# Splitting the first load of x and of the weights in two, moving the load of the mix, and moving the retrieval's weight splits behind the last norm

## The chip, the cores and the metric

The kernel runs on one core of a Trainium2 chip. The metric is the device time in microseconds (us) of one execution; three timed runs of the kernel before the change are given below, with one profiled execution. Engines are named as in the profile: PE (TensorE), ACT (ScalarE), DVE (VectorE), POOL (GpSimd) and SP (SyncE, which here issues DMAs). PEld is the weight load of PE.

## What is computed

One decoder block for 512 tokens of width 1024, all in float32:

```
u = rms_norm(x, norm_mix_g)
z = u @ w_in                                   # 1024 x 3328
o = concat(diff_attention(z[:, :1536]), rwkv7_mix(z[:, 1536:]))
h = x + o @ w_out
q = rms_norm(h, norm_ffn_g) @ peer_w_q         # retrieval: 8 heads, 16 of 128 x 128 keys
h = h + sum over the 16 best experts of gate * gelu(u . exp_u) * exp_v
h = h + sigmoid(rms_norm(h, norm_ple_g) @ ple_gate_w) * (p @ ple_proj_w)
out = rms_norm(h, norm_final_g)
```

In `rwkv7_mix` the projected columns are first blended with those of the token before, `zs = z + (prev - z) * mu`; `mu` (rw_mu) is "the mix" of the change. `diff_attention` needs sine and cosine tables of the positions (the rotary tables).

## The kernel before

Matmuls work on pairs of fp32r tiles: every operand is split into `hi` (a rounded copy, made by ACT, line 133) and `lo` (the rest, made by DVE or POOL, line 143, or line 145 where a gain is multiplied in). A product is three matmuls: hi by hi, hi by lo, lo by hi (lines 217 to 219).

**The first projection.** `mixers` computes columns of z in groups of four token blocks at a time, contracting over eight blocks k of 128 rows. The groups come in the order k (512 columns), l (256 columns, the low-rank inputs), r, v, then the attention's columns. `proj_steps` takes weights from `stream`, which fetches two blocks k in one DMA of 512 KB into a raw tile (`wraw`, three buffers), splits them block by block into `whi` and `wlo` (two buffers of each, two blocks to a buffer) and yields them one after the other. In the first group x itself is still to be loaded: `columns(k)` loads two blocks of the transposed x (`xt`, 512 KB) and splits them into `uhi` and `ulo`; the list `begin` says after which block k the next such load, the squares of x and the row scales are written.

**The shift.** `shift_group` gets the results of a group: ACT copies each block out of PSUM with its row scale into `zz` (line 446), then SP issues two or three DMAs for each block (lines 455 to 460, 11 for a group) that shift it by one token, and POOL computes the blend in three instructions for each block (lines 461 to 464). `mu` is loaded when the group is set up (line 438), as one row that is written to all 128 partitions, 256 KB.

**The rotary tables.** `rope_tables` (lines 349 to 424) works on tiles of 128 x 32 with a long chain of small DVE instructions. `lambdas` (lines 330 to 346) makes two small DVE sums of four short loads (`lam`). Both are written after the groups k, l, r and v and have no order of their own.

**What sets the order.** The program is written in one order and a scheduler then gives every engine its own fixed list, by its own estimate of when inputs are ready. `behind(i, first)` holds instruction i after `first` on the same engine's list without a wait on the chip. An edit in one place can thus move instructions elsewhere. The queue of SP is one list too: a DMA whose buffer is not yet free holds up all behind it.

**The output projection and the norm.** `out_proj` multiplies by `w_out` (lines 253 to 255); after the last block's two halves `norm(b)` is called for the blocks: ACT squares (line 1061), DVE adds the two sums (1649), ACT takes the root (123), DVE the reciprocal (124) and the two halves of the normed rows `xn` (1653), PE transposes them (159), ACT and DVE split them into `u2hi` and `u2lo`. Then `retrieve` multiplies the weights `peer_w_q`, streamed in the same way, by them (lines 1113 to 1115). The first four pairs of its blocks are split by ACT and DVE, later ones by ACT and POOL.

## Time and profile before

| | us |
|---|---|
| median of 3 runs | 1800.03 |
| lowest and highest | 1797.09, 1800.13 |
| the profiled execution, its own time | 1795.69 |
| its span, first to last instruction | 1794.0 |
| PE busy in the span | 1691.8 (94%) |
| DVE busy | 1397.3 (78%) |
| ACT, POOL busy | 751.5, 647.3 |

The profiled execution lies 4.34 us under the median and 1.7 us over its own span. Times in rows are from the start of the span. The stretch from 0 to about 111 us is the projection of the groups k, l, r, v and the first attention columns, 400 to 455 us the output projection and the norm, 455 to 600 us the retrieval, and the rest the experts.

### The profile page before, as it was taken

To read this page: it belongs to the slowest core of one execution; us is meant where nothing else is said; L and a number is where in the kernel's file an instruction comes from. 1 tells how busy PE (TensorE), PEld (TensorE's weight loads), DVE (VectorE), ACT (ScalarE), POOL (GpSimd) and SP (SyncE) were. 2 spreads that over 40 slices of the span, in tenths; PEclk is the share of its full clock that TensorE was granted. 3 is DMA by queue.
4 is the path that set the end of the run, shared out by engine and by line. 5 is a ranking of instruction groups with operands and counts; after the bars stand their busy time and mean duration, and the time that the engine had idled before them with its cause. 6 is when DMAs were issued, how large, how long until landed. Compare 5 with 4: busy or idle time off the path is not lost.

```text
span 1794.0 us, 30877 instructions
## 1 busy us (share of the span) xinstructions
PE 1691.8 (94%) x11642; PEld 1447.2 (81%) x11642; DVE 1397.3 (78%) x3004; ACT 751.5 (42%) x1358; POOL 647.3 (36%) x574
## 2 busy tenths in 40 slices
PE   7899978989889879999999999999999999999998
PEld 5767667667677879997777888888999989989986
DVE  5486858774499979878888888888888888888785
ACT  5345523343456654444444333333333333333363
POOL 3460120212278840001111233335545455555520
PEclk9899966899999989999999999999999999999999
DMA  7444353414522434455665677778989898989881
GB/s 230 147 128 118 106 130 87 111 27 165 188 82 81 139 102 132 137 188 198 210 208 190 221 267 235 262 266 299 315 301 316 301 319 301 313 308 315 304 321 47
DMA packets 150426, 363.86 MB, mean 203 GB/s; under 512 B 43922, under 2 KB 58510, under 8 KB 150148
## 3 DMA queue, kind: packets, MB, share of 16 engines
q1 hardware_dynamic: 113412, 227.65, 38.9%
q0 software_dynamic: 36864, 134.23, 22.1%
q8 instruction: 91, 1.49, 0.3%
q14 instruction: 59, 0.48, 0.1%
HBM read 332.61 MB, written 21.36 MB: 197 GB/s over the span
## 4 chain that ended last, share of the span: by engine, by line
PE 67%; DVE 24%; ACT 4%; issue 2%; DMA 2%; POOL 1%; SPq 0%; DVEq 0%; ACTq 0%; POOLq 0%
PE po L1395 22%; PE phid L1253 9%; PE phid L1255 9%; PE phid L1254 8%; PE pg L1364 3%; ACT whi L133 2%; DVE wlo L143 2%; PE acc L217 2%; PE acc L218 2%; PE acc L219 2%; DVE ids L1202 1%; DVE rest L1079 1%; DVE sol_p L630 1%; DVE wlo L145 1%; DVE jj L1352 1%
## 5 line engine op out<-in xcount | busy, mean ns | idle before, releaser
L143 DVE TENSOR_TENSOR wlo<-wraw,whi 128x1024 fp32r<-128x1024 f32 x245 | 299.6, 1223 | 144.7 <-ACT whi L133 144.6
L133 ACT ACTIVATE whi<-wraw 128x1024 fp32r<-128x1024 f32 x276 | 291.4, 1056 | 166.6 <-PE phid L1254 68.5
L1253 PE MATMUL phid<-u2dhi,whi 128*128 128x384 f32 x1024 | 349.1, 341 | 5.7 <-ACT row L1262 5.7
L1255 PE MATMUL phid<-u2dhi,wlo 128*128 128x384 f32 x1024 | 346.1, 338 | 5.5 <-POOL wlo L143 5.5
L1254 PE MATMUL phid<-u2dlo,whi 128*128 128x384 f32 x1024 | 345.6, 338 | 0.0
L1418 POOL DMA_INDIRECT row<-in_peer_u_dram,idx x128 | 190.0, 1485 | 408.0 <-DVE row L1430 219.4
L1418 POOL DMA_INDIRECT row<-in_peer_v_dram,idx x128 | 186.0, 1453 | 276.3 <-DVE h L1434 194.4
L1395 PE MATMUL po<-whi,clo 128*128 128x512 f32 x768 | 243.1, 398 | 1.4
L1395 PE MATMUL po<-whi,chi 128*128 128x512 f32 x768 | 243.3, 398 | 1.2 <-ACT row L1262 1.2
L1395 PE MATMUL po<-wlo,chi 128*128 128x512 f32 x768 | 241.4, 395 | 0.0
L1253 PEld LDWEIGHTS phid<-u2dhi,whi 128*128 128x128 f32 x1024 | 193.5, 189 | 10.8 <-ACT row L1262 6.6
L1255 PEld LDWEIGHTS phid<-u2dhi,wlo 128*128 128x128 f32 x1024 | 193.4, 189 | 6.1 <-POOL wlo L143 6.1
L1254 PEld LDWEIGHTS phid<-u2dlo,whi 128*128 128x128 f32 x1024 | 193.7, 189 | 3.7
L1395 PEld LDWEIGHTS po<-whi,clo 128*128 128x128 f32 x768 | 143.0, 188 | 41.9 <-DVE clo L145 8.7
L1395 PEld LDWEIGHTS po<-wlo,chi 128*128 128x128 f32 x768 | 144.4, 188 | 33.6
L133 ACT ACTIVATE chi<-gelu 128x384 fp32r<-128x384 f32 x128 | 67.3, 526 | 240.6 <-DVE gelu L1372 121.4
L1434 DVE SCALAR_TENSOR_TENSOR h<-row,ids,h 128x1024 f32<-128x1024 f32 x128 | 163.9, 1280 | 1.5
L1395 PEld LDWEIGHTS po<-whi,chi 128*128 128x128 f32 x768 | 140.9, 188 | 25.6 <-ACT row L1262 1.5
L1262 ACT ACTIVATE gelu<-phid 128x384 f32<-128x384 f32 x86 | 42.4, 493 | 266.4 <-PE phid L1255 244.8
L1430 DVE SCALAR_TENSOR_TENSOR row<-row,xn 128x1024 f32<-128x1024 f32 x128 | 153.6, 1219 | 0.0
L143 POOL TENSOR_TENSOR wlo<-wraw,whi 128x1024 fp32r<-128x1024 f32 (+1 forms) x46 | 80.0, 1752 | 111.3 <-ACT whi L133 111.3
L218 PE MATMUL acc<-wlo,uhi 128*128 128x512 f32 (+1 forms) x224 | 89.7, 401 | 10.7 <-DVE wlo L145 10.7
(452 smaller groups left out, 2866.1 us busy)
## 6 DMA issues: line engine op xcount, KB each, us to landing
wraw<-in_peer_uT_dram SPq DMA_DIRECT2D x128, 512.0 KB
wraw<-in_peer_v_dram SPq DMA_DIRECT2D x128, 512.0 KB
wraw<-in_w_in_dram SPq DMA_DIRECT2D x24, 512.0 KB
wraw<-in_peer_w_q_dram SPq DMA_DIRECT2D x16, 512.0 KB
ahead<-row SPq DMA_DIRECT2D x42, 192.0 KB
gelu<-ahead SPq DMA_DIRECT2D x42, 192.0 KB
wraw<-in_w_out_dram SPq DMA_DIRECT2D x8, 512.0 KB
zz<-zz SPq DMA_DIRECT2D x12, 224.0 KB
```

The costliest lines, as they stand in the source:

```text
L133: self.last_hi = nc.scalar.activation(hi, src, AF.Copy, **({} if g is None else {"scale": g}))
L143: self.last_lo = eng.tensor_tensor(lo[s], src[s], hi[s].bitcast(F32), op=OP.subtract)
L218: nc.tensor.matmul(o, hi[:, k, s], wlo, start=False, stop=False)
L1253: nc.tensor.matmul(ps, whi[:, s], hi[:, k, :], start=(k == 0), stop=False)
L1254: nc.tensor.matmul(ps, whi[:, s], lo[:, k, :], start=False, stop=False)
L1255: nc.tensor.matmul(ps, wlo[:, s], hi[:, k, :], start=False, stop=(k == KC - 1))
L1262: nc.scalar.activation(g, ps, AF.Gelu)
L1364: nc.tensor.matmul(ps[:, t], jj[:, t], gi[:, i, t], start=i == 0, stop=i == 1)
L1395: nc.tensor.matmul(outs[b, e], lhs[:, s], rhs[:, 512 * e:512 * e + 512], start=(c == 0 and rhs is vhi and lhs is chi), stop=(c == NKEY - 1 ...
L1418: nc.gpsimd.indirect_dma_start(out=row, out_offset=None, in_=a["peer_u" if kind == "U" else "peer_v"], in_offset=bass.IndirectOffsetOnAxis ...
L1430: nc.vector.scalar_tensor_tensor(row, row, 1.0, xn0, op0=OP.mult, op1=OP.mult, accum_out=hid0[:, k:k + 1])
L1434: nc.vector.scalar_tensor_tensor(acc0, row, hid0[:, k:k + 1], acc0, op0=OP.mult, op1=OP.add)
```

## The change

Three edits. (1) For the first pair of blocks alone, x and the weights are loaded as two DMAs of 256 KB each instead of one of 512 KB, and x is split block by block: the first half of x before the product of block 0, the second after it. (2) The load of `mu` for the first group is written later, after the row scales; for the other groups it stays where it was. (3) In `out_proj` the norm of block 2 is written behind the last half product instead of ahead of it, and in `retrieve` the splits of the first three pairs of weight blocks are held behind the last block's norm: ACT's part behind its square root, DVE's part behind the last half of `xn`.

```diff
@@ rms
-        nc.scalar.activation(r, ss, AF.Sqrt, bias=self.eps, scale=1.0 / D)
+        self.rooted = nc.scalar.activation(r, ss, AF.Sqrt, bias=self.eps, scale=1.0 / D)
@@ fetch
-        i = self.nc.sync.dma_start(raw[:, :n] if len(src.shape) == 2 else
-                                   raw[:, :n].rearrange("p (k n) -> p k n", k=src.shape[1]), src)
+        if not self.fetches:
+
+            for k in range(2):
+                m = n // 2
+                i = self.nc.sync.dma_start(raw[:, k * m:k * m + m], src[:, k])
+        else:
+            i = self.nc.sync.dma_start(raw[:, :n] if len(src.shape) == 2 else
+                                       raw[:, :n].rearrange("p (k n) -> p k n", k=src.shape[1]), src)
@@ shift_group
-        nc.sync.dma_start(mu[:, :n], bcast_row(self.a["rw_mu"][:, g0:g0 + n], n))
+
+        def load_mu():
+            nc.sync.dma_start(mu[:, :n], bcast_row(self.a["rw_mu"][:, g0:g0 + n], n))
...
-        return zs, consume
+        return zs, consume, load_mu
@@ mixers
-            columns(0)
-            begin = {0: [lambda: columns(2)], 2: [lambda: columns(4)], 4: [lambda: columns(6)],
+
+            xt0 = self.p4("xt", [128, 2, T])
+
+            def column(k):
+                nc.sync.dma_start(xt0[:, k], a["xT"][k * 128:k * 128 + 128, :])
+                self.split(hi[:, k], lo[:, k], xt0[:, k])
+            column(0)
+            begin = {0: [lambda: column(1), lambda: columns(2)], 2: [lambda: columns(4)], 4: [lambda: columns(6)],
...
+                if zs:
+                    load_mu()
+                else:
+                    begin[7].append(load_mu)
@@ out_proj
-                            for x in ((0, 1, 2), (3,))[i]:
+                            for x in ((0, 1), (2, 3))[i]:
@@ retrieve
+                        if cg == 0 and k in (2, 4):
+
+                            self.behind(self.last_hi, self.rooted)
+                            self.behind(self.last_lo, self.normed)
@@ norm
-                    nc.vector.scalar_tensor_tensor(xn[:, d], h[b][:, d], r, g[:, d], op0=OP.mult, op1=OP.mult)
+                    self.normed = nc.vector.scalar_tensor_tensor(xn[:, d], h[b][:, d], r, g[:, d], op0=OP.mult,
+                                                                 op1=OP.mult)
```

What the scheduler makes of it, at three places. Numbers behind a tile's name only tell its buffers apart.

SP at the program's start, before (`xt` is the transposed x, `wraw` raw weights):

```order
L914 DMA g_mix_112<-in_norm_mix_gT_dram 128x8
L923 DMA xt_119<-in_xT_dram 128x2x512
L438 DMA mu_123<-in_rw_mu_dram 128x512
L169 DMA wraw_129<-in_w_in_dram 128x2x512
L923 DMA xt_135<-in_xT_dram 128x2x512
L169 DMA wraw_165<-in_w_in_dram 128x2x512
```

and in the changed kernel, with the later place of `mu` ahead of the weights of group l (`wraw_377`):

```order
L922 DMA g_mix_112<-in_norm_mix_gT_dram 128x8
L948 DMA xt_119<-in_xT_dram 128x512
L173 DMA wraw_128<-in_w_in_dram 128x512 x2
L948 DMA xt_119<-in_xT_dram 128x512
L931 DMA xt_138<-in_xT_dram 128x2x512
L175 DMA wraw_168<-in_w_in_dram 128x2x512
...
L87 DMA b_rw_r_k_304<-in_rw_r_k_dram 128x512
L446 DMA mu_123<-in_rw_mu_dram 128x512
L175 DMA wraw_377<-in_w_in_dram 128x2x256
```

The load of `mu` no longer stands between the first x and the first weights, and the first matmul needs one half of each.

DVE in the groups l to v, before (`wlo` of 128x256 are the weights of group l, those of 128x512 from `wlo_546` on those of r; h2, h1y, x0 and the like belong to the rotary tables):

```order
L145 SCALAR_TENSOR_TENSOR wlo_408<-wraw_405,g_mix_112,whi_407 128x256 x2
L394 TENSOR_SCALAR h2_935<-h2_935 128x32
L395 TENSOR_TENSOR x0_933<-x0_933,h2_935 128x32
...
L384 TENSOR_SCALAR x0q_965<-x0_933 128x32
L145 SCALAR_TENSOR_TENSOR wlo_440<-wraw_437,g_mix_112,whi_439 128x256 x2
L387 SCALAR_TENSOR_TENSOR h2y_939<-h2q_941,h2y_939 128x32
...
L417 TENSOR_SCALAR x0_933<-x0_933 128x32
L145 SCALAR_TENSOR_TENSOR wlo_472<-wraw_469,g_mix_112,whi_471 128x256 x2
L458 MEMSET zz_501 1x256
L145 SCALAR_TENSOR_TENSOR wlo_546<-wraw_543,g_mix_112,whi_545 128x512 x2
```

and in the changed kernel (`wlo_646` is the last pair of group r, `wlo_761` the first of group v):

```order
L145 SCALAR_TENSOR_TENSOR wlo_444<-wraw_441,g_mix_112,whi_443 128x256 x2
L145 SCALAR_TENSOR_TENSOR wlo_476<-wraw_473,g_mix_112,whi_475 128x256 x2
L466 MEMSET zz_505 1x256
L145 SCALAR_TENSOR_TENSOR wlo_550<-wraw_547,g_mix_112,whi_549 128x512 x2
...
L145 SCALAR_TENSOR_TENSOR wlo_646<-wraw_643,g_mix_112,whi_645 128x512 x2
L361 CAST posf_924<-pi32_922 128x4
L367 TENSOR_TENSOR ang_935<-posf_924,freq_926 128x32
...
L346 SCALAR_TENSOR_TENSOR lams_1001,lame_1000<-lam_995 128x64
L145 SCALAR_TENSOR_TENSOR wlo_761<-wraw_758,g_mix_112,whi_760 128x512 x2
L414 SCALAR_TENSOR_TENSOR h1y_958<-h1_954,h1y_958 128x32
```

The whole chain of the rotary tables has moved out of group l. It now stands behind the last weights of group r, 35 rows of it (with the two `lams`) ahead of the first weights of group v and the rest behind them; no line of the edit names it. SP's loads of the positions and of `lam` moved with it, from ahead of group k's shift to behind the second load of group v's weights; the last of them (the half of `lam` that the second `lams` reads) stands behind the third.

DVE around the norm of the last block, before (`wlo` are the retrieval's weights, `xn_4918` the last block's normed rows):

```order
L1059 TENSOR_TENSOR h3_4485<-accr_4886,h3_4485 128x512
L143 TENSOR_TENSOR u2lo_4497<-tps_4879,u2hi_4496 128x4x128
L143 TENSOR_TENSOR wlo_5123<-wraw_5120,whi_5122 128x1024
L1649 TENSOR_TENSOR r_4914<-ss_ffn_4479 128x1
L143 TENSOR_TENSOR wlo_5033<-wraw_5030,whi_5032 128x1024
L143 TENSOR_TENSOR wlo_5093<-wraw_5090,whi_5092 128x1024
L124 RECIPROCAL r_4914<-r_4914 128x1
L1653 SCALAR_TENSOR_TENSOR xn_4918<-h3_4485,r_4914,b_norm_ffn_g_4489 128x512 x2
L143 TENSOR_TENSOR u2lo_4497<-tps_4921,u2hi_4496 128x4x128
```

and in the changed kernel:

```order
L1077 TENSOR_TENSOR h3_4489<-accr_4869,h3_4489 128x512
L143 TENSOR_TENSOR u2lo_4501<-tps_4904,u2hi_4500 128x4x128
L1671 TENSOR_TENSOR r_4918<-ss_ffn_4483 128x1
L143 TENSOR_TENSOR u2lo_4501<-tps_4911,u2hi_4500 128x4x128
L124 RECIPROCAL r_4918<-r_4918 128x1
L1675 SCALAR_TENSOR_TENSOR xn_4922<-h3_4489,r_4918,b_norm_ffn_g_4493 128x512 x2
L143 TENSOR_TENSOR wlo_5037<-wraw_5034,whi_5036 128x1024
L143 TENSOR_TENSOR wlo_5067<-wraw_5064,whi_5066 128x1024
L143 TENSOR_TENSOR u2lo_4501<-tps_4925,u2hi_4500 128x4x128
```

Three weight splits no longer stand between the last sum of h and `xn`; two now stand between `xn` and the last block's `u2lo`. ACT's list changes in the same way: two `whi` ahead of the root go behind it, and three now stand between the root and the last block's `u2hi`. On PE the transposes of block 2, which stood among the last three products of the output projection, now stand behind them. On SP the load of the fourth pair of `peer_w_q` moves behind that of the keys, and the loads of the next column group behind the two copies of `u2hi` and `u2lo`.

## Rows read from the trace of the kernel before

**Rows 1.** The page's chain of work that ended last, shares by engine.

```profile
PE 67%; DVE 24%; ACT 4%; issue 2%; DMA 2%; POOL 1%; SPq 0%; DVEq 0%; ACTq 0%; POOLq 0%
```

**Rows 2.** The waits of PE over the whole span, longest in total first; columns are the waiting line, what it waited for, total us, times, longest.

```profile
PE acc L218 <- DVE wlo L145: 10.7, 2, 7.2
PE acc L217 <- ACT whi L133: 9.5, 1, 9.5
PE tps L159 <- DVE xn L1653: 6.3, 1, 6.3
```

**Rows 3.** ACT in order of time at the start of the span: start, duration, instruction, and in brackets the idle time before it and what ended it.

```profile
5.06 1.06 ACT L133 ACTIVATE uhi<-xt 128x1024 fp32r<-128x1024 f32 x1 [2.99 <-DMA xt<-in_xT_dram]
8.71 1.33 ACT L133 ACTIVATE whi<-wraw,g_mix 128x512 fp32r<-128x512 f32 x2 [2.59 <-DMA wraw<-in_w_in_dram]
10.00 1.06 ACT L133 ACTIVATE uhi<-xt 128x1024 fp32r<-128x1024 f32 x1
12.70 1.06 ACT L133 ACTIVATE uhi<-xt 128x1024 fp32r<-128x1024 f32 x1
```

**Rows 4.** Two windows of 1 us at the start: busy time of each engine, the granted clock, the share of the DMA engines and GB/s (the last number).

```profile
5.00:6.00 1.00, 0.00 (x0) 0.00 (x0) 0.00 (x0) 0.94 (x1) 0.88 (x6) 1.00 0.82 162
8.00:9.00 1.00, 0.00 (x0) 0.00 (x0) 0.00 (x0) 0.29 (x1) 0.32 (x2) 1.00 1.06 410
```

**Rows 5.** PE in order of time, its first matmuls.

```profile
9.48 1.22 PE L217 MATMUL acc<-whi,uhi 128*128 128x512 f32 x2 [9.48 <-ACT whi L133]
```

**Rows 6.** PE in order of time: the first matmul of group l, its two waits, the first matmul of group r (128x512 again) and the first of group v.

```profile
33.42 0.28 PE L217 MATMUL acc<-whi,uhi 128*128 128x256 f32 x1
...
42.95 0.38 PE L218 MATMUL acc<-wlo,uhi 128*128 128x256 f32 x1 [3.46 <-DVE wlo L145]
...
55.13 0.58 PE L218 MATMUL acc<-wlo,uhi 128*128 128x256 f32 x1 [7.23 <-DVE wlo L145]
...
59.56 0.63 PE L217 MATMUL acc<-whi,uhi 128*128 128x512 f32 x1
...
82.38 0.39 PE L217 MATMUL acc<-whi,uhi 128*128 128x512 f32 x1
```

**Rows 7.** A window in group l; the last three numbers are the granted clock as a share of 2.4 GHz, the DMA share and GB/s.

```profile
54.00:58.00 4.00, 2.87 (x13) 2.88 (x14) 2.83 (x9) 0.12 (x1) 0.00 (x0) 0.50 0.27 81
```

**Rows 8.** DVE in order of time, groups l to v: rotary rows, weight splits, and the second sum of `lam`.

```profile
35.81 1.27 DVE L394 TENSOR_SCALAR h<-h 128x32 f32<-128x32 f32 x1
...
42.42 1.89 DVE L145 SCALAR_TENSOR_TENSOR wlo<-wraw,g_mix,whi 128x256 fp32r<-128x256 f32 x2
...
52.15 0.18 DVE L387 SCALAR_TENSOR_TENSOR x<-x0q,x 128x32 f32<-128x32 f32 x1
...
54.50 0.18 DVE L417 TENSOR_SCALAR x<-x 128x32 f32<-128x32 f32 x1
...
73.46 1.41 DVE L145 SCALAR_TENSOR_TENSOR wlo<-wraw,g_mix,whi 128x512 fp32r<-128x512 f32 x2 [5.02 <-ACT whi L133]
75.72 0.23 DVE L340 SCALAR_TENSOR_TENSOR lams<-lam 128x64 f32<-128x64 f32 x1 [0.85 <-DMA lam<-in_lam_k_dram]
```

**Rows 9.** POOL in order of time: first and last of the 12 shift instructions of group k, then of the 12 of group l.

```profile
35.59 1.45 POOL L461 TENSOR_TENSOR zz<-zz 128x512 f32<-128x512 f32 x1 [27.27 <-DMA zz<-zz]
...
50.88 1.29 POOL L464 TENSOR_TENSOR zs<-zz 128x512 f32<-128x512 f32 x1
61.18 1.09 POOL L461 TENSOR_TENSOR zz<-zz 128x256 f32<-128x256 f32 x1 [9.01 <-DMA zz<-zz]
...
72.24 0.74 POOL L464 TENSOR_TENSOR zsl<-zz 128x256 f32<-128x256 f32 x1
```

**Rows 10.** SP's queue in order of time: the first DMA of group k's shift, and the load of group l's last weights behind the shift's 11 DMAs (a row that merges three loads; its start is that of the first).

```profile
32.23 0.59 SPq L455 DMA_DIRECT2D zz<-zz  x1
...
40.22 4.49 SPq L169 DMA_DIRECT2D wraw<-in_w_in_dram  x3
```

**Rows 11.** ACT in order of time: the split of group l's last pair of weights.

```profile
43.32 0.91 ACT L133 ACTIVATE whi<-wraw,g_mix 128x256 fp32r<-128x256 f32 x2 [5.83 <-DMA wraw<-in_w_in_dram]
```

**Rows 12.** DVE in order of time at the norm: the last sum of h, two merged weight splits, the last block's normed rows.

```profile
449.07 0.68 DVE L1059 TENSOR_TENSOR h<-accr,h 128x512 f32<-128x512 f32 x1
...
451.64 2.36 DVE L143 TENSOR_TENSOR wlo<-wraw,whi 128x1024 fp32r<-128x1024 f32 x2
...
454.11 1.42 DVE L1653 SCALAR_TENSOR_TENSOR xn<-h,r,b_norm_ffn_g 128x512 f32<-128x512 f32 x2
```

**Rows 13.** ACT in order of time at the norm: the last squares, the root, the first split of the last block.

```profile
449.94 0.62 ACT L1061 ACTIVATE sqo<-h 128x512 f32<-128x512 f32 x1
...
452.45 0.28 ACT L123 ACTIVATE r<-r,eps 128x1 f32<-128x1 f32 x1
456.13 0.60 ACT L133 ACTIVATE u2hi<-tps 128x512 fp32r<-128x512 f32 x1 [3.39 <-PE tps L159]
```

**Rows 14.** PE in order of time at the norm: the first transposes of block 2, the last product of the output projection, the transposes of the last block, the second product of the retrieval.

```profile
447.17 0.63 PE L159 MATMUL tps<-ident,xn 128*128 128x128 f32 x4
...
448.22 0.48 PE L255 MATMUL accr<-rhi,olo 128*128 128x512 f32 x1
455.01 1.94 PE L159 MATMUL tps<-ident,xn 128*128 128x128 f32 x8 [6.30 <-DVE xn L1653]
...
457.50 0.79 PE L1114 MATMUL accq<-u2lo,whi 128*128 128x512 f32 x1
```

More of the change, by code (lines that the diff above doesn't have):

```diff
@@ L940, in mixers @@
             for tag, c0, n in (("k", 512, 512), ("l", 1536, 256), ("r", 0, 512), ("v", 1024, 512)):
-                z, consume = self.shift_group(rs, (lambda: self.small.tile([128, 256], F32, name="zsl", bufs=NB))
+                z, consume, load_mu = self.shift_group(rs, (lambda: self.small.tile([128, 256], F32, name="zsl", bufs=NB))
                                               if tag == "l" else (lambda: p2("zs")), c0, n)
+                if zs:
+                    load_mu()
+                else:
+                    begin[7].append(load_mu)
                 if tag == "v":
```

## The prediction

> **What bounds the kernel now.** I read the page's chain first: two thirds of it is PE, a quarter DVE [rows 1]. So a microsecond that PE waits in an early stage is a microsecond of the total, unless something later is paced by another clock; from the retrieval on the lists of all engines are the same in both programs, and each stage starts from the one before. Then PE's waits [rows 2]: three of the longest are where the change works. PE starts at 9.5 us, when the first weights are split; in group l it waits twice, 10.7 us, for DVE's half of the weights; at the last norm it waits 6.3 us for `xn`. Then each place by itself, in order of time.
>
> **The start.** ACT could split x from 5.06 us on, when 516 KB had landed (the gains and the first x, 512 KB), but the first weights only at 8.71 [rows 3]. Between them stands the load of `mu`: in that microsecond the DMAs moved 162 KB, later 410 KB in one [rows 4]. In the changed kernel the same 516 KB are the gains, half of x and half of the weights. So `whi` starts at about 5.1 to 5.5 (one more DMA is issued), takes half of 1.33 [rows 3], and the first matmul comes at 5.9 in place of 9.48 [rows 5]; the next one needs `wlo`, half of a 1.41 us pair [rows 8], at 6.6. Before, two matmuls were done in 1.22 us by 10.7 [rows 5], now one by 6.6, and one costs some 0.6 us at that clock: the lead is 3.4 us. The second halves are 512 KB more, 1.3 us at the later rate, and another 2 us of splits: there by 8.9, while 12 matmuls from 6.6 on last beyond 9.3 even at the 0.237 us that group r's 96 take each (22.8 us [rows 6]). Later loads come no later than before, as nothing was added ahead of them, and `mu` is wanted only at POOL's second shift instruction. Bounds: 3.6 us, or 1.9 if the early start keeps PE at its lower clock twice as long (3 us of matmuls at half speed, 1.6 us lost). I take 3.4.
>
> Rows 3 also show what halving a DMA costs: two loads of 512 KB (one x, one weights) end 2.70 us after the two before them, 1.35 each, so they overlap and the queue pays by bytes.
>
> [...]
>
> **Group l.** From its first matmul at 33.42 to the first of group r at 59.56 are 26.1 us [rows 6]; its 96 matmuls of half the width, 0.118 us each, need 11.3. The rest is waits, 3.46 and 7.23, and the lower clock behind them (0.50 in the second [rows 7]; the last 20 matmuls take 4.4 us). Both waits are for `wlo` rows that stand on DVE's list behind rotary rows. These are slow there: from 35.81 to 52.15 there are 25 of them in 14.5 us (the `wlo` pair left out), 0.58 us each, while POOL runs group k's shift from 35.59 to 52.17; then 13 take 2.4 us, 0.19 each [rows 8, 9]. In the changed order none stands in group l. What is late next: group l's last weights. SP issues them behind the shift's 11 DMAs, which begin 1.2 us before the group does and take 8.0; ACT gets them at 43.32, that is 9.9 us after the group's start [rows 6, 10, 11]. This is paced by the group's own start, so it moves with it. PE would want them after 6 of 8 blocks, at 8.5. Half of ACT's 0.91 and half of 1.89 for `wlo` beside POOL [rows 8, 11] let it go on at 11.3, four matmuls having run ahead; 20 more are 2.4 us, or 4.3 at the lower clock. Group l lasts 13.7 to 15.6 us: 10.5 to 12.4 us less. A wait of some 2.5 us is near the first one of 3.46, after which the clock fell: I take 11.5.
>
> **Where the rotary rows go.** Now 35 of them stand between the last weights of group r and the first of group v, and hold the latter, for which PE waits. Group r runs 22.8 us, 59.56 to 82.38 [rows 6]; its last weights are split 15.3 us after its start (73.46 + 1.41 [rows 8]), which SP's queue paces from the end of group l, so this moves along. Alone, 35 rows of 0.19 take 6.6 us: to 21.9; half a pair of `wlo` to 22.6. Just in time. POOL's shift of group l has 12 instructions; here it queues behind that of group k, which is 16.6 us long and starts 2.2 us into group l [rows 6, 9], so it begins 4 us into group r and, at the 11.8 us that it took (61.18 to 72.98 [rows 9]), ends at 16: a fraction of a microsecond of overlap. The second `lams` needs the last load of `lam`, now issued behind the load that waits for that last split; one load ahead of it and 3.1 us from issue to use (40.22 to 43.32 [rows 10, 11]) bring it at about 20, before its turn. Price: 0 to 1.5 us, I take 0.5. If the cover is gone, the dear rows price it, below.
>
> **The norm.** Before, the last product ends at 448.70, `xn` starts at 454.11 and PE at 455.01 [rows 12, 14]. On that path stand three weight splits on DVE, two of them the merged 2.36 us [rows 12], and three on ACT around the squares (449.94) and the root (452.45) [rows 13]. In the changed lists block 2's transposes, 0.63 us for four [rows 14] and overlapping the product ahead, no longer delay the last product: it ends near 447.8. From there: sum 0.7, squares 0.8 behind one `u2hi` of 0.6 that overlaps, add and root 0.9 behind the other `u2hi`, reciprocal 0.5 behind `u2lo`, half of 1.42: `xn` at 451.5, 3.4 us earlier. Then the splits are late: ACT runs three `whi` of 1 us before the last block's `u2hi` (453.7), DVE two `wlo` of 2.36 together before `u2lo`, 452.2 to 454.6, and 0.6 for that one: the retrieval's second product at 455.2 against 457.50 [rows 14]. Gain 2.3 us; 3.4 if the product went by `xn` alone, 1.0 if broken waits keep the clock low longer. The fourth pair of weights, now loaded behind the keys, is wanted 16.8 us later; that hides it. The next group's loads, now behind two copies, are wanted 22 us later, which covers them too, by less.
>
> **Sum.** 3.4 + 11.5 - 0.5 + 2.3 = 16.7 us off 1795.7, the profiled execution: 1779.0. That execution lies 4.3 us under the median of the runs shown, so I forecast 1783 for a median. Bounds of the terms: 3.6 + 12.4 + 3.4 = 19.4 (1776 from the profiled execution, 1781 from the median) and 1.9 + 10.5 - 1.5 + 1.0 = 11.9 (1784 and 1788).
>
> **Rivals.**
> - The wait moves to group v. If POOL's shift of group l starts later than I work out and runs 8 us into the chain, those 8 us hold 14 rows at 0.58, the other 21 take 4: 12 us, a wait of 5, and 2 to 3 us of lower clock behind it. Gain 9: 1791. For it speaks the narrow margin; against it that POOL has nothing else to do. Chance 0.17.
> - The halved loads gain little. One load of 256 KB takes 3.1 us from issue to use (40.22 to 43.32 [rows 10, 11]); if two were paid in sequence from the first issue at about 1.3, the weights' half would come at 7.5 and the first matmul at 8.2: a lead of 1, and 1785.5. Rows 3, with 1.35 us for twice as much, speak against it. Chance 0.08.
> - The lead is taken back: DVE's next long stretch, group v's, sets PE's pace whatever PE did before, and only the norm's 2 us stay: 1796 to 1798. Against it: that stretch starts from splits that wait for PE. Chance 0.06.
> - Slower. The 35 rows meet POOL throughout: at 0.58 they take 20.3 us, a wait of 14, with lower clock 17; at 1.27 each (the dearest rows, as 35.81 [rows 8]) 44 us, a wait of 38, and the total is 1783 + 38 + 2 = 1823. It turns slower from about 0.7 us a row. POOL's 12 rows cannot cover that, unless group l's shift is held to the end of group r. Chance 0.03.
>
> The slow rows beside POOL's work agree with a rule of the Trainium skill, "SBUF — State Buffer", section Who interferes with whom: DVE and POOL share one port pair as an exclusive lock, and the loser blocks for the whole instruction. Read strictly, every row beside POOL would wait for one POOL instruction, which is the dear end of the last rival; the mean of 0.58 us in rows 8 is against that, since several rows pass between two blocks.
>
> **How the numbers follow.** The forecast (1781 to 1788) has 0.66. The range takes in the gain bound of the profiled execution and the wait at v: 1776 to 1793. By cases, faster by over 0.2% (3.6 us, about what a measurement of this kernel can tell from no change) has 0.91: forecast, moved wait, halved loads. Within 0.2%: 0.06. Slower: 0.03.
>
> **What would show it.** First matmul at about 6 us; group l 14 to 15 us long with one wait of about 2 us, for weights that SP loaded late; rotary rows of 0.2 us behind group r's last split and PE's wait at group v under 1.5 us; the wait for `xn` near 3 us, and a second one of 1 to 2 us ahead of the retrieval's second product. Wrong: rotary rows of 1.2 us, a PE wait over 4 us at group v, or a lead that is smaller at 120 us than at 60.

## The result, and the profile after

| | before | after |
|---|---|---|
| median of 4 runs, us | 1800.08 | 1787.05 |
| lowest and highest | 1797.09, 1800.84 | 1785.08, 1788.12 |
| ratio, with its 95% interval | | 0.9925 [0.9913, 0.9938] |
| the profiled execution, its own time | 1795.69 | 1786.43 |

The change takes 13.0 us off the median. The forecast was 1783, from a sum of 16.7. The two profiled executions are only 9.3 us apart, since that of before lies 4.4 under its median and that of after 0.6 under its own.

What follows speaks of a **lead**: how much earlier a matmul starts than the same matmul in the trace of before. PE in order of time in the trace after: its first matmul, the two waits of group l, the first matmuls of groups r and v, the first product with `lw` (plw), the last block's transposes and the retrieval's second product.

```profile
5.58 0.80 PE L223 MATMUL acc<-whi,uhi 128*128 128x512 f32 x1 [5.58 <-ACT whi L133]
...
40.24 0.73 PE L223 MATMUL acc<-whi,uhi 128*128 128x256 f32 x4 [1.75 <-ACT whi L133]
...
41.80 0.39 PE L224 MATMUL acc<-wlo,uhi 128*128 128x256 f32 x1 [0.83 <-DVE wlo L145]
...
44.62 0.39 PE L223 MATMUL acc<-whi,uhi 128*128 128x512 f32 x1
...
67.20 0.39 PE L223 MATMUL acc<-whi,uhi 128*128 128x512 f32 x1
...
100.97 2.07 PE L514 MATMUL plw<-w_up,lw 65*128 65x512 f32 x2 [8.78 <-DVE lw L510]
...
443.72 1.29 PE L159 MATMUL tps<-ident,xn 128*128 128x128 f32 x8 [3.02 <-DVE xn L1675]
...
447.16 0.80 PE L1136 MATMUL accq<-u2lo,whi 128*128 128x512 f32 x1 [0.94 <-DVE u2lo L143]
```

Against [rows 5, 6, 14] the lead is 3.9 at the first matmul (3.7 through group k), 15.2 at the first of group v (82.38 - 67.20), and 10.3 at the retrieval's second product (457.50 - 447.16). Between these it fell: plw came at 111.10 before, which is a lead of 10.1. So the start and group l gave what was forecast, and 5 us of it were lost in group v: not at its beginning, where PE has no wait, but at its end, where PE waits 8.78 us for `lw` in place of 3.97.

ACT after, at the start, beside [rows 3]: the halves of x and of the weights.

```profile
3.96 0.63 ACT L133 ACTIVATE uhi<-xt 128x512 fp32r<-128x512 f32 x1 [1.89 <-DMA xt<-in_xT_dram]
4.80 0.72 ACT L133 ACTIVATE whi<-wraw,g_mix 128x512 fp32r<-128x512 f32 x1 [0.21 <-DMA wraw<-in_w_in_dram]
...
7.51 0.71 ACT L133 ACTIVATE whi<-wraw,g_mix 128x512 fp32r<-128x512 f32 x1
```

The place of the loss is group v. First the trace of before there (rows not shown ahead), view by view in order of time: SP (the first DMA of group r's shift), POOL (the shift's first and last instruction), DVE (the first of 13 rows `knx`, an inverse root for the keys; the four products `kk`; the copy of `lw` out of PSUM), and PE (plw).

```profile
81.19 0.56 SPq L455 DMA_DIRECT2D zz<-zz  x1
```

```profile
85.40 1.29 POOL L461 TENSOR_TENSOR zz<-zz 128x512 f32<-128x512 f32 x1 [12.43 <-DMA zz<-zz]
...
103.17 1.30 POOL L464 TENSOR_TENSOR zs<-zz 128x512 f32<-128x512 f32 x1
```

```profile
104.94 0.17 DVE L94 TENSOR_SCALAR knxh<-knr 128x32 f32<-128x32 f32 x1
...
108.23 2.50 DVE L484 TENSOR_TENSOR kk<-kk,knx 128x512 f32<-128x512 f32 x4
110.64 0.41 DVE L502 COPY lw<-ptl 64x256 f32<-64x256 f32 x1
```

```profile
111.10 1.56 PE L506 MATMUL plw<-w_up,lw 65*128 65x512 f32 x2 [3.97 <-DVE lw L502]
```

The same in the trace after: SP (a constant, group v's last weights, the shift's first DMA), POOL, and DVE from the rotary rows on.

```profile
63.48 0.43 SPq L87 DMA_DIRECT2D b_rw_ln_b<-in_rw_ln_b_dram  x1
...
67.87 0.38 SPq L175 DMA_DIRECT2D wraw<-in_w_in_dram  x1
68.34 0.57 SPq L463 DMA_DIRECT2D zz<-zz  x1
```

```profile
74.41 1.29 POOL L469 TENSOR_TENSOR zz<-zz 128x512 f32<-128x512 f32 x1 [14.30 <-ACT whi L133]
...
92.74 1.31 POOL L472 TENSOR_TENSOR zs<-zz 128x512 f32<-128x512 f32 x1
97.11 1.26 POOL L469 TENSOR_TENSOR zz<-zz 128x512 f32<-128x512 f32 x1 [3.06 <-DMA zz<-zz]
```

```profile
62.16 0.17 DVE L361 CAST posf<-pi 128x4 f32<-128x4 int32 x1 [0.59 <-DMA pi<-in_positions_dram]
...
66.28 0.23 DVE L346 SCALAR_TENSOR_TENSOR lams<-lam 128x64 f32<-128x64 f32 x1
...
66.43 1.41 DVE L145 SCALAR_TENSOR_TENSOR wlo<-wraw,g_mix,whi 128x512 fp32r<-128x512 f32 x2
...
89.52 1.26 DVE L94 TENSOR_SCALAR knxh<-knr 128x32 f32<-128x32 f32 x1
...
91.44 1.26 DVE L98 TENSOR_SCALAR knx<-knxi 128x32 int32<-128x32 int32 x1
...
95.93 4.65 DVE L492 TENSOR_TENSOR kk<-kk,knx 128x512 f32<-128x512 f32 x4
100.50 0.41 DVE L510 COPY lw<-ptl 64x256 f32<-64x256 f32 x1
```

Before, the shift's first DMA went out 1.2 us ahead of group v's first matmul and POOL began 3.0 behind it. After, the load of v's last weights waits for the buffer that v's first split frees (66.43 + 1.41), the shift stands behind it on SP's list, and the constants' loads, issued from 62.5 on, are still on their way (from 68 to 71.1 the trace still has 78 packets of 512 bytes to 2 KB; in e3_consts below, which moves those loads away, it has none). The shift's first DMA goes out 1.1 behind group v's start, and POOL begins 7.2 behind it. (The profile names ACT as what released POOL here, since a `whi` ended just then; in the second trace of this kernel, e6_again below, it names the DMA of `zz`.) So POOL is still at work when DVE comes to `knx` (89.52 to 94), and has begun the next shift beside `kk` (97.11). The 13 `knx` rows take 5.5 us in place of 2.4 and `kk` 4.65 in place of 2.50, and `lw` comes 33.3 us after group v's start in place of 28.3. The theory to test: **PE's lead was cut back by a late shift, by way of POOL and DVE.** Rivals: DVE's stretch in group v takes what it takes whatever POOL does; or the loss is the clock of one execution.

### The profile page after: what moved, and what is told of

It reads as the page before. It is cut to its first block, busy times and chain, and to the rows that moved or that the text cites. A ratio compares the mean times of both kernels' runs of the same rounds, so it can differ in the third digit from the quotient of the medians.

```text
span 1784.7 us, 30882 instructions
## 1 busy us (share of the span) xinstructions
PE 1690.9 (95%) x11642; PEld 1444.6 (81%) x11642; DVE 1399.7 (78%) x3005; ACT 750.5 (42%) x1359; POOL 648.3 (36%) x574
## 4 chain that ended last, share of the span: by engine, by line
PE 65%; DVE 24%; ACT 4%; issue 2%; DMA 2%; SPq 1%; POOL 1%; DVEq 0%; ACTq 0%; POOLq 0%
PE po L1417 22%; PE phid L1275 9%; PE phid L1277 9%; PE phid L1276 9%; PE pg L1386 3%; DVE wlo L143 2%; ACT whi L133 2%; DVE ids L1224 1%; DVE rest L1097 1%; DVE sol_p L638 1%; DVE wlo L145 1%; DVE jj L1374 1%; DVE si L1095 1%; PE accr L259 1%; DVE si L1099 1%
## 5 line engine op out<-in xcount | busy, mean ns | idle before, releaser
L223 PE MATMUL acc<-whi,uhi 128*128 128x512 f32 (+1 forms) x224 | 86.4, 392 | 7.3 <-ACT whi L133 7.3
```

The source lines that it names most:

```text
L223: nc.tensor.matmul(o, hi[:, k, s], whi, start=(k == 0), stop=False)
```

## The experiments

Each kernel was timed in five rounds beside before (medians 1798.9, 1799.0 and 1799.1 in three sets; the row of after is the four runs above), and its ratio is against before; 0.001 is 1.8 us. In the table, lead is from the traces, each of a single execution: in group k, at group v's start, just behind plw, and behind the norm (475 us). POOL and lw are the first instruction of group r's shift and the copy of `lw`, in us after the first matmul of group v; then PE's longest wait for `lw`.

| kernel | k | v | plw | 475 | POOL | lw | wait | ratio |
|---|---|---|---|---|---|---|---|---|
| before | 0 | 0 | 0 | 0 | 3.0 | 28.3 | 4.0 | 1 |
| after | 3.7 | 15.2 | 10.1 | 8.9 | 7.2 | 33.3 | 8.8 | 0.9925 |
| e6_again | 2.3 | 14.3 | 8.4 | 6.4 | 7.5 | 34.0 | 9.0 | 0.9931 |
| e8_late | 2.4 | 14.5 | 5.3 | 6.1 | 10.3 | 37.9 | 11.8 | 0.9951 |
| e3_consts | 3.1 | 14.6 | 12.3 | 17.9 | 6.1 | 30.7 | 6.3 | 0.9914 |
| e4_shift | 2.8 | 14.3 | 12.6 | 10.3 | 2.4 | 29.1 | 4.8 | 0.9905 |
| e11_shift_again | 2.9 | 15.2 | 14.7 | 14.1 | 2.9 | 29.4 | 4.9 | 0.9911 |
| e12_whole_start | -0.7 | 9.0 | 10.9 | 6.3 | 1.8 | 28.0 | 3.5 | 0.9932 |
| e1_start | 3.2 | 14.3 | 9.9 | 9.7 | 7.4 | 32.6 | 7.9 | 0.9931 |
| e5_rotary | -0.3 | 11.4 | 9.1 | 9.8 | 5.8 | 30.4 | 6.1 | 0.9937 |
| e9_mu_early | 0.2 | 9.7 | 8.4 | 4.4 | 5.5 | 30.1 | 5.8 | 0.9935 |
| e7_no_split | 1.5 | 1.4 | 0.5 | -4.1 | 3.8 | 29.1 | 4.1 | 0.9984 |
| e10_lw_first | 3.2 | 14.7 | 21.1 | 11.7 | 1.9 | 23.9 | 0.6 | 0.9904 |

Intervals of the ratios are about 0.0016 to either side (2.9 us), so that the difference of two of them is known to some 4 us; those that decide are given below.

### Freeing the shift: e4_shift, e11_shift_again, e3_consts

```diff
@@ late_consts (load_bcast keeps its DMA in self.loaded)
-        nc.sync.dma_start(self.g_up, a["rw_g_up"])
+        self.behind(nc.sync.dma_start(self.g_up, a["rw_g_up"]), self.shifted_r)
         self.ln_g = self.load_bcast(pool, "rw_ln_g", 512)
+        self.behind(self.loaded, self.shifted_r)   # ln_b and subln likewise
@@ mixers (shift keeps its last DMA in self.shifted)
                 if tag == MARK:
                     self.mark = self.last_hi
+                    self.shifted_r = self.shifted
+                if tag == "v":                     # not in e3_consts
+                    self.behind(self.fetches[-1], self.shifted_r)
```

> The changed kernel with five loads (the gate's g_up, three broadcast constants, group v's last weights) issued behind group r's shift DMAs in place of ahead of them. Theory: of the 15 us of lead that PE has at the start of group v, five are lost because group r's shift reaches POOL late (7.2 us after group v's start, before 3.0), so that POOL's work stands beside DVE's small rows and the four kk rows ahead of lw. Here the shift's first DMA goes out at about 66.7 in place of 68.3 and lands in 3.4 us in place of 5.1: POOL's shift starts at about 70.5, ends near 90, the rows ahead of lw take 0.2 us each and the four kk rows 2.5 in place of 4.65, PE's wait for lw is 4 to 5 us in place of 8.8, the lead at that place is 14 us and the total 1783. Rival: DVE's stretch in group v takes what it takes, from splits that wait for PE and for POOL's own pace; the wait for lw stays at 8 to 9 and the total at 1787.

Measured 1783.54, 0.9905 [0.989, 0.9921]. The trace of e4_shift: SP, POOL, DVE and PE.

```profile
67.56 0.56 SPq L466 DMA_DIRECT2D zz<-zz  x1
```

```profile
70.51 2.78 POOL L472 TENSOR_TENSOR zz<-zz 128x512 f32<-128x512 f32 x1 [9.48 <-ACT whi L133]
...
90.02 1.61 POOL L475 TENSOR_TENSOR zs<-zz 128x512 f32<-128x512 f32 x1
```

```profile
94.80 2.50 DVE L495 TENSOR_TENSOR kk<-kk,knx 128x512 f32<-128x512 f32 x4
97.22 0.41 DVE L513 COPY lw<-ptl 64x256 f32<-64x256 f32 x1
```

```profile
97.68 1.22 PE L517 MATMUL plw<-w_up,lw 65*128 65x512 f32 x1 [4.80 <-DVE lw L513]
```

With POOL's shift over at 91.6, `kk` takes 2.50 us again and the wait is back at 4.8. The lead behind plw was 12.6, not the 14 expected; the time came as the theory said (1783), and not as the rival did (1787).

> The kernel with the freed shift once more, unchanged, beside the next two on the same chip: 1783.5 as in its first run, with PE's wait for lw under 5 us and a lead of 12 to 13 at 118 us.

Measured 1781.65, 0.9911 [0.9896, 0.9926]; wait 4.9, lead behind plw 14.7. So the freed shift has 0.9905 and 0.9911, the changed kernel 0.9925 and 0.9931: some 3.6 us between them, repeated.

> The changed kernel with four constants' loads (g_up and three broadcast rows) issued behind group r's shift DMAs and group v's next weights; group v's last weights stay ahead of the shift, as in the changed kernel. It divides the run that freed the shift altogether. If the constants' bytes are what delays the shift's landing, the first shift DMA goes out at about 68.5 as in the changed kernel and POOL starts at about 72.5 (74.4 there, 70.5 with both parts moved); PE's wait for lw is 6 to 7 us (8.8 there, 4.8), total 1785. If it is the place behind group v's last weights that costs, POOL starts at 74, the wait for lw is 8 to 9 and the total 1787.

Measured 1782.91, 0.9914 [0.9897, 0.993]. The wait for `lw` lies between, at 6.3, though POOL starts only 0.5 us earlier, at 73.89 (6.1 behind group v's start, 7.2 in after). From the shift's first DMA to POOL's start it is 5.2 us, where the changed kernel has 6.1 and 5.6 and e4_shift 3.0: the constants count for less than 1 us, the load just ahead of the shift for 2.2. Of the 2.5 us that the wait is shorter, 2.15 are `kk`, which runs before POOL's next shift begins (98.13):

```profile
96.08 2.50 DVE L495 TENSOR_TENSOR kk<-kk,knx 128x512 f32<-128x512 f32 x4
```

The times do not separate this kernel from e4_shift.

### Delaying it: e8_late

```diff
@@ shift
+            for _ in range(2 if b == 0 and g0 == 0 else 1):
-            nc.sync.dma_start(zp[1:113, :n], z[0:112, :n])
-            nc.sync.dma_start(zp[113:128, :n], z[112:127, :n])
+                nc.sync.dma_start(zp[1:113, :n], z[0:112, :n])
+                nc.sync.dma_start(zp[113:128, :n], z[112:127, :n])
```

> The changed kernel with the two DMAs of group r's first shifted block issued twice (the same bytes to the same place), which holds the rest of that shift back by 3 to 4 us; three of DVE's splits in group v change places with their neighbours, all of the rows ahead of lw stay ahead of it. Theory (the late shift stands beside DVE's rows ahead of lw): POOL's shift starts near 78 in place of 74.4 and ends near 98; all of the knx rows and the kk rows are beside it, lw comes 2 to 4 us later, PE's wait for lw is 11 to 13 us and the total 1789.5 to 1791. Rival (DVE's stretch is paced by PE's own splits): wait and total as in the changed kernel, 8.8 and 1787.

Measured 1789.8, 0.9951 [0.9935, 0.9966]. POOL and DVE of this kernel:

```profile
77.67 1.28 POOL L470 TENSOR_TENSOR zz<-zz 128x512 f32<-128x512 f32 x1 [16.47 <-DMA zz<-zz]
```

```profile
98.54 6.73 DVE L493 TENSOR_TENSOR kk<-kk,knx 128x512 f32<-128x512 f32 x4
```

`kk` stands beside POOL's next shift altogether: 6.73. The wait is 11.8, and the lead behind plw falls to 5.3. Earlier or later, the shift moves PE's wait with it; the rival of a fixed stretch on DVE falls.

### A second trace: e6_again

No edit.

> The changed kernel once more, unchanged, for a second trace of the same instructions. What belongs to the change repeats: a lead over before of 3.7 us at group k, 15 at the end of group l, 10 from plw on, PE's wait for lw 8 to 9. What belongs to the single execution does not: the 3 us that were lost at 340 to 350 us, where the granted clock fell to 0.65 and 0.50 and no wait grew, and the 1.5 us at 545 to 555. Total 1787.

Measured 1785.67, 0.9931 [0.9915, 0.9947]. The loss at plw repeats (14.3 to 8.4, wait 9.0). But the expectation was wrong in its second half: the loss of 3 us at 325 to 365 repeats as well (8.8 to 5.3), and the 1.6 at 545 to 556. Both are taken up at the end.

### The parts by themselves: e5_rotary, e1_start, e2_norm, e7_no_split, e9_mu_early, e12_whole_start

e5_rotary is before with the rotary rows held by hand (`mark_lo` is group r's last `wlo`):

```diff
-        nc.vector.tensor_copy(pf, pi32)
+        self.behind(nc.vector.tensor_copy(pf, pi32), self.mark_lo)
```

> Before with the rotary rows held behind group r's last split and nothing else changed: the term of group l by itself. The lead is 0 through group k and 10 to 12 us at the end of group l. If the loss at lw belongs to the moved rows and the late shift, 6 to 7 us are left there and the total is 1793 to 1794; if the loss needs the start's lead as well (a fixed later pace that only a lead of 10 meets), nothing is lost at lw and the total is 1789; if group v's stretch on DVE sets PE's pace whatever PE did before, 1799 to 1800.

Measured 1787.94, 0.9937 [0.9921, 0.9952], that is 11.3 us less. Group l gave 11.7 in its trace, and 2.3 were lost at plw: nearest to the second reading, which had nothing lost there.

e1_start is after without the norm's part:

```diff
-                            for x in ((0, 1), (2, 3))[i]:
+                            for x in ((0, 1, 2), (3,))[i]:
@@ retrieve
-                        if cg == 0 and k in (2, 4):
-                            self.behind(self.last_hi, self.rooted)
-                            self.behind(self.last_lo, self.normed)
```

> The start of the changed kernel with the norm of before (the third of block 3's weights and the order around the norm are as they were). If the start's loads and the rotary rows bring what the trace of the changed kernel shows up to the norm, this kernel leads before by 3.7 us through group k, by 15 us at the end of group l, by about 10 us from the first product plw on, and by 8 to 10 at 440 us; at the norm PE waits 6.3 us for xn as before and nothing is added. Total 1789 to 1790, some 2.5 above the changed kernel. Rival: the norm's gain is given back behind it (lower clock in the retrieval); then this kernel takes the changed kernel's time, 1787.

Measured 1787.5, 0.9931 [0.9915, 0.9947]: by the times, the norm is worth 0 to 1 us in the changed kernel, which no measurement here tells from none; the rival's side.

e2_norm is before with that part alone (the two hunks above, the other way round).

> Before with the norm's part alone (block 2's sum behind the last product, the retrieval's splits behind the root and xn). The lead is 0 up to 440 us, 2.5 us at the retrieval's second product, as in the changed kernel, and 1.2 to 2.5 stay: 1797.5 to 1799 against a median of 1800. Rival: the lead is given back by 470 us to a lower granted clock and the total is 1800.

Measured 1797.88, 0.9995 [0.9985, 1.0005]: 0.9 us, which this measurement can't tell from none. In its trace the lead rises by 2.5 at the norm (0.4 to 2.9), and 1.5 of that are left at 475 us.

e7_no_split is after with whole first loads (`fetch` as before, `columns(0)` in place of `column(0)` and `column(1)`), mu late.

> The changed kernel with the first x and weights loaded whole, as before; mu late and the norm's part as changed. In this kernel's list the rotary rows stand in group l again, as before: the halved first loads are what moved them. Lead 1 to 1.6 us through group k (mu's 256 KB are out of the way), no gain in group l, the same 1 to 1.6 behind it, and 1 us of the norm: 1797 to 1798. If the rotary rows' place were of no account and the loads were what counts in group l, the lead would be over 10 us there and the total under 1790.

Measured 1796.65, 0.9984 [0.9972, 0.9995]. In this kernel's list the rotary rows stand in group l, and PE waits 9.7 us there for `wlo`. So it is the halved first loads that make the scheduler put those rows elsewhere; that, not the loads' own time, is most of the change.

e9_mu_early is after with mu's load where it was:

```diff
-                if zs:
-                    load_mu()
-                else:
-                    begin[7].append(load_mu)
+                load_mu()
```

> The changed kernel with mu loaded where it was before, between the first halves of x and of the weights; the halves, the rotary rows' place and the norm as changed. The start: 256 KB that move slowly stand ahead of the first weights again, so the first matmul comes 1 to 1.6 us later than the changed kernel's 5.6 (the kernel with mu late and whole loads led by 1.6), and PE leads by 2 to 2.5 us at group k, by 13 at the end of group l. What follows depends on the place of the loss: if DVE's rows ahead of lw, delayed by the late shift, set PE's pace at plw, most of that microsecond was lost there anyway: 1787 to 1788. If a lead at the start comes through whole, 1788.5.

Measured 1787.33, 0.9935 [0.9922, 0.9948]. At group v's start it is 4.6 to 5.5 us behind the two traces of the changed kernel (9.7 against 15.2 and 14.3); behind plw 0 to 1.7, and in time some 1 us. What PE has gained at the start is lost at plw.

e12_whole_start is e4_shift with the start of before and the rotary rows held as in e5_rotary.

> The kernel with the freed shift, but with the start of before (first x and weights whole, mu ahead of them) and the rotary rows held behind group r's last split by hand: the start's term by itself, in a kernel in which the shift is not late. If the start's lead of 3 us then comes through, this kernel takes 3 us more than the kernel with the freed shift: 1786 to 1787, with a lead of 0 at group k, 11.4 at the end of group l and 9.5 to 10.5 at 118 us. If the start is worth nothing (a later pace that PE meets in any case), it takes the same 1783.5. In the changed kernel, where the shift is late, rotary rows alone and rotary rows with the start differed by only 1 us.

Measured 1787.16, 0.9932 [0.9918, 0.9946], against 0.9911 and 0.9905 for the same kernel with the new start: 4 to 5 us, and 1.7 to 3.8 by the lead behind plw. Where the shift is not late, the start is worth about what was forecast (3.4); in the changed kernel (0.9931 without the norm, against 0.9937 for the rotary rows alone) it is worth 1, and 0.8 by the lead (9.9 against 9.1). The times alone, known to some 4 us, do not separate the two cases; the leads point the same way.

### What is late next: e10_lw_first

On top of e4_shift, `rw_keys` leaves the `knx` and `kk` rows to a function that is called behind the copies of `lw` and `lg`:

```diff
@@ rw_prepare
-        nc.vector.tensor_copy(st["lg"], pt[:, 2, :])
+        copied = nc.vector.tensor_copy(st["lg"], pt[:, 2, :])
+        if b == 0:
+            self.scale_kk(copied)     # knx rows, held behind the copy, and kk
```

> The kernel with the freed shift, and in group v DVE's copies of lw and lg ahead of the thirteen knx rows and the four kk rows, which don't need them (nor they these). If those rows are what PE waits for at plw, the copies run at about 92.5 in place of 97.2, PE's wait for lw falls from 4.8 to 1.5 us or less (PE now comes to plw five matmuls earlier, which it has left over behind it), the lead at 118 us is 15.5 to 16.5 in place of 12.6, and the total is 1780, 3 to 4 us under the freed shift alone. Rival: the next stage waits for DVE's kk and e_ex chain, which is 0.7 us later now; then PE's waits for DVE between 118 and 150 us grow by what was won and the total is 1783 to 1784.

Measured 1781.99, 0.9904 [0.9886, 0.9922]: not measurably faster than e11_shift_again on the same chip (0.9911). DVE and PE of this kernel:

```profile
91.54 0.41 DVE L517 COPY lw<-ptl 64x256 f32<-64x256 f32 x1
...
97.53 6.87 DVE L147 SCALAR_TENSOR_TENSOR wlo<-wraw,g_mix,whi 128x512 fp32r<-128x512 f32 x4
```

```profile
92.00 1.13 PE L523 MATMUL plw<-w_up,lw 65*128 65x512 f32 x2 [0.56 <-DVE lw L517]
...
115.94 0.50 PE L226 MATMUL acc<-wlo,uhi 128*128 128x512 f32 x1 [2.51 <-DVE wlo L147]
...
117.72 0.63 PE L579 MATMUL ptr<-ident,be 128*128 128x128 f32 x4 [1.28 <-DVE be L558]
```

The wait for `lw` is gone and the lead is 21.1 behind plw, more than expected. Then PE waits for a `wlo` and for `be`, which stand beside POOL's next shift (`wlo` 1.72 each here), and at 140 us of before's time the lead is 15.0, where the freed shift alone has 14.7 and 12.6. The rival's outcome, one stage on. The versions with the freed shift beat both kernels, with 1782 to 1784; this one adds nothing that can be measured.

## Why the prediction was right, and where it was not

The time came out 4 us above the forecast and inside the range, with the larger terms right and one term missing. That it stayed under 1788 in spite of the missing term is in part luck: that bound was made of a small start, a long group l, late rotary rows and a small norm, and had no loss behind group v's start in it.

**The start.** Forecast 3.4; 3.7 and 2.3 through group k in the two traces. The first matmul came at 5.58 (forecast 5.9) and the second half of the weights was split from 7.51 on (forecast: by 8.9). So the second rival, in which two loads are paid in sequence, the weights' half comes at 7.5 and the first matmul at 8.2, did not come true: ACT began on that half at 4.80.

**Group l.** It lasts 14.9 us (29.74 to 44.62; forecast 13.7 to 15.6) and has waits of 1.75 and 0.83 (forecast 2.5): 11.3 gained, against 11.5. e5_rotary gives 11.3 in the times, alone.

**The rotary rows.** They took 4.3 us, 62.16 to 66.43, and held group v by nothing (by 0.6 in the second trace); forecast 0.5. POOL's shift of group l ended at 60.1, as worked out.

**The step that failed** stands in the first paragraph: that what PE gains stays, since "each stage starts from the one before", and its twin under the third rival, that group v's stretch on DVE "starts from splits that wait for PE". Part of it does not: what its rows take depends on group r's shift, by SP's queue, the DMAs and POOL, and of these POOL had only 11.0 us of lead (85.40 - 74.41) where PE had 15.2. The other traces agree: POOL's lead at this place and PE's lead behind plw are 7.7 and 5.3 in e8_late, 8.7 and 9.1 in e5_rotary, 10.2 and 10.9 in e12_whole_start, 14.9 and 12.6 in e4_shift, 15.4 and 14.7 in e11_shift_again. The exception is e10_lw_first, which took the slowed rows out of the way of `lw` (15.9 and 21.1). I priced the moved rows up to group v's first weights, and not what is queued on SP behind the load that waits for that split. The sum lacks a term of -5.1, 15.2 to 10.1 (-5.9 in the second trace). With the shift freed it is -1.7 and -0.5 (e4_shift, e11_shift_again), with a later shift -9.2 (e8_late). The prediction named "a lead that is smaller at 120 us than at 60" as what would prove it wrong, and that is what the trace shows: 15.1 and 10.1. It also named a wait of PE over 4 us at group v: there is none for the rotary rows, for which it was meant, and one of 8.8 for `lw`.

**The rivals.** A wait of 5 us more in group v was forecast as a rival, with chance 0.17, for POOL's shift of group l beside the rotary rows. The size came true (8.8 in place of 4.0, for `lw`), in another place and from another cause. The third rival was right in kind: a lead can be taken back by DVE in group v. It was wrong in degree, since that takes the lead above what SP and POOL have, not all of it.

**The norm.** Forecast 2.3; 2.5 at the retrieval's second product, with the waits as forecast (3.0 for `xn`, then 0.54 and 0.94). Then 1.4 are given back. Windows of the norm, the third number from the end being the granted clock; after, then before:

```profile
443.72:448.00 4.28, 2.76 (x11) 1.74 (x12) 4.28 (x6) 2.27 (x4) 0.00 (x0) 0.73 0.76 258
448.00:452.00 4.00, 4.00 (x10) 3.07 (x10) 1.28 (x2) 1.06 (x1) 0.00 (x0) 0.50 1.05 376
```

```profile
455.01:460.00 4.99, 4.99 (x15) 3.67 (x16) 1.90 (x3) 1.19 (x2) 0.00 (x0) 0.52 0.85 280
460.00:464.00 4.00, 4.00 (x18) 3.19 (x18) 0.00 (x0) 0.02 (x1) 0.00 (x0) 1.00 1.02 298
```

Before, PE had idled once, for 6.3 us, and is back at the full 2.4 GHz by 460. After, it idles three times and stays at 1.2 GHz until 452. That is the lower bound of the forecast, 1.0; the times (0 to 1) agree with it. The traces of the changed kernel lose another 1.6 us at 545 to 556 (last section), so that by then nothing of the norm's 2.5 is left in them.

**The sum.** By the trace of after 3.7 + 11.5 - 5.1 + 1.1 is 11.2 (lead at the end of k, to group v, at plw, across the norm up to 475 us); beside that, 1.0 is won between plw and 325 us, and 3.3 and 1.6 are lost at 325 to 365 and 545 to 556. By the times: rotary rows 11.3, start 1, norm 0 to 1, together 13, where only the first is clear of the noise. The traces say less than the times since the trace of before is one of its fastest executions.

## What to carry to other kernels

A gain of PE at the start was worth here about as much as the lead of POOL, on which the work ahead of `lw` depends: note not only when PE, but when SP, POOL and DVE reach the next stage, and compare. When instructions are moved in front of a split, follow the buffer that this split frees to the load that waits for it, and to all that is queued behind that load. And a small edit to a load can move other work through the scheduler: here that moved work was some 11 of the 13 us.

## What was not expected of the hardware

**DVE rows beside POOL.** Before, the 13 `knx` rows took 2.4 us in sum; after, 5.5. Of the five that ran while POOL's shift was still on (89.52 to 94.05), three took 1.14 to 1.26 and two, each right behind one that had waited, 0.17 and 0.19; the rows behind 94.05 took 0.2 again. The three ended at 90.78, 92.70 and 94.10, each 0.05 behind the end of one of POOL's instructions (90.73, 92.66, 94.05). The four `kk` rows of 128x512 took 0.6 each alone and 1.7 each beside POOL throughout (6.73 for four), which is what one of POOL's instructions takes there. The Trainium skill, "SBUF — State Buffer", Who interferes with whom, tells of a port pair that DVE and POOL share as an exclusive lock, the loser blocked for a whole instruction. The traces agree with that for each row that waits, and show that about every second small row slips through.

**The length of a stretch at the lower clock.** From about 325 to 365 us of before's time the kernels shown run the same instructions in the same order (but for two neighbouring matmuls of e3_consts), and PE's five longest waits there (0.2 to 1.0 us) are the same to 0.1 us. Three windows each of before, of after and of e3_consts:

```profile
347.00:350.00 3.00, 3.00 (x37) 2.36 (x36) 0.96 (x4) 1.09 (x4) 0.00 (x0) 0.53 0.34 55
356.00:359.00 3.00, 3.00 (x39) 1.32 (x39) 1.10 (x2) 0.00 (x0) 2.22 (x2) 0.76 0.82 208
359.00:362.00 3.00, 2.94 (x68) 2.37 (x67) 1.91 (x4) 0.00 (x0) 0.00 (x0) 1.00 0.07 11
```

```profile
331.00:334.00 3.00, 3.00 (x20) 2.88 (x19) 2.73 (x7) 0.60 (x1) 0.00 (x0) 0.65 0.00 0
340.00:343.00 3.00, 3.00 (x31) 2.17 (x28) 0.29 (x1) 0.87 (x2) 0.00 (x0) 0.50 0.27 46
346.00:349.00 3.00, 3.00 (x9) 1.25 (x6) 1.34 (x3) 0.21 (x1) 2.14 (x3) 0.50 0.25 55
```

```profile
335.00:338.00 3.00, 3.00 (x11) 2.24 (x12) 1.82 (x4) 1.37 (x3) 0.00 (x0) 0.50 0.32 78
338.00:341.00 3.00, 3.00 (x9) 1.07 (x5) 1.29 (x2) 0.00 (x0) 2.42 (x3) 0.52 0.73 201
341.00:344.00 3.00, 3.00 (x71) 2.26 (x72) 0.69 (x1) 0.00 (x0) 0.79 (x1) 1.00 0.54 143
```

PE is busy in these windows, and granted 1.2 GHz for some 10 us before, 7 in e3_consts, and 14 after, beside another dip there (331 to 333) that before did not have. Between 325 and 365 us the lead thus moves by -3.3 after, -3.5 in e6_again, +1.9 in e3_consts and -5.7 in e12_whole_start, and it is why a lead at the end of one trace (8 us after, 17 in e3_consts) says less than the ratio.

The 1.6 us at 545 to 556 are of the same kind. PE waits once there, for `rest`, 2.1 us before and 2.0 after; behind the wait the clock is granted in full before, and not after:

```profile
555.00:558.00 3.00, 3.00 (x15) 2.41 (x14) 3.00 (x24) 1.18 (x2) 2.00 (x2) 1.00 0.54 169
```

```profile
546.00:549.00 3.00, 3.00 (x12) 2.43 (x11) 3.00 (x24) 1.18 (x2) 0.82 (x2) 0.65 0.52 154
```

The nine traces that have the norm's part together with halved loads or a late mu all lose 1.5 to 1.6 us there, the four that do not (e1_start, e2_norm, e5_rotary, e12_whole_start) lose nothing. What sets the length of such a stretch, or brings it, was not settled.
